# A float32-split encoder trunk on one core: branch B in another order, wider spacing of attention heads, the softmax scaling on another engine, two output blocks interleaved, and tiles written in the order in which the transposes read them

## The chip, the cores and the metric

The kernel runs on one core of one Trainium2 chip. The metric is the device time of one execution in microseconds (us), lower is better.

## The reference, cut to what matters

Two layers (DEPTH = 2), 256 tokens, 2048 channels, float32:

```python
h = rmsnorm(x, pre_norm_g[l])
proj = einsum('bsd,dn->bsn', h, w_in[l])       # 35 blocks of 512 columns
qa,ka,va, qb,kb,vb, qc,kc,vc, za,zb,zc, gates = split(proj)
ya = neighbourhood_attention(qa, ka, va, rpb[l])   # branch A: 8 heads
yb = gqa_attention(rope(rmsnorm(qb)), rope(rmsnorm(kb)), vb)  # branch B: 8 heads, 2 for k and v
yc = dilated_mixture(qc, kc, vc)                   # branch C: 12 heads, 4 sums
merged = ga*((ya*silu(za)) @ w_branch_a) + gb*((yb*silu(zb)) @ w_branch_b) \
       + gc*((yc*silu(zc)) @ w_branch_c)           # ga, gb, gc = sigmoid(gates + b_gate)
x = x + rmsnorm(merged @ w_out[l], post_norm_g[l])
```

## The kernel before, in words

**The stream of products.** All large products run as one list, `stream`, of steps (block, kc). A block (`Blk`) is one product with 512 output columns, and a step takes 256 of its input channels for all 256 tokens. For each step SP loads 512 KB of weights (`emit_raw`, L189), ScalarE rounds them to the fast float32 format (`emit_hi`, tile wh, L195), VectorE forms the remainder (`emit_lo`, tile wl, L200), and TensorE runs 12 matmuls of 128x512 (`run_half` and `mm3`, L170 to L172): two halves of the tokens (T = 0, 1), two groups of 128 channels, and three products each, wh by the high part, wl by the high part, wh by the low part. `ahead` issues the loads some six steps ahead, wh three and wl two steps ahead.

**The order of blocks of a layer.** z, q, k, v of branch C; z, q, k, v of branch A, twice; z of B (blocks 20, 21), k and v of B (8), q of B (6, 7); then four times `merge`: three gate blocks and the products by w_branch_a, w_branch_c and w_branch_b; then four output blocks (`out_block`) by w_out. An output block's steps kc = 0 to 7 read the merged tiles mT 0 to 3, two steps each.

**Everything else rides in slots.** After each step `slot()` is called once: it evacuates up to one finished accumulator, moves every active job (a Python generator) to its next `yield`, and may start one new job. Light jobs (`later`) go first; a heavy job, one attention head, starts only when no light job waits and the count `cool` that the head before has set is down to zero. Engines take their instructions in program order, so the slot in which a piece is issued sets what stands before and behind it on its engine.

**Turns.** Results come token-major (tokens on the partitions) and are needed channel-major. `turn` transposes 32x32 blocks on VectorE (L148, into tile tt), writes tt to DRAM and reads it back as tx (L153, L157 on SP, two slots apart each). The program has 168 such transposes: 88 of 128x512 that read q, k, z (tile tok) or the merged tile (g), less four of half the width, and 80 that read softmax results (tile sp). Each reads its source with a stride of four elements (`p (h b j) -> p h j b`). `tr_job` is a turn and the split of the result into a high and a low part. Of a turn's tiles the writers are: `evac_qk` (L326, ScalarE), `evac_z` (L353 ScalarE, L354 VectorE), `evac_p` (L605, L607 VectorE) for the merged tile, `softmax` (L369, exp on ScalarE) for p, and `rope` (L513, L521, L523) for q and k of branch B.

**A head** (`head_job`): six 128x256 matmuls into sc; `softmax`: maximum (L364), for B times a factor (L366), exp; one slot later `norm`: 1/sum (L377, L378) and p times it (L380, VectorE); two slots later the turn of p; after it the split into pp (L130, L132), two slots, six matmuls into o, and `gate` (L384). The last head of a group of four splits the result into yT. In branch B the heads are queued by the `then` of the `tr_job` of q, in the slot in which that job issues its last pieces. `evac_qb` evacuates q of B: squares of four heads (L531), a factor (L533), `rope`, L546.

## Time and profile before

| | |
|---|---|
| median of 3 runs | 2043.8 us (2043.03 to 2046.01) |
| the profiled execution | 2045.3 us; from its first to its last instruction 2043.2 us |
| mean granted TensorE clock | 0.994 of full speed |
| TensorE matmuls | 9098, busy 2014.1 us |
| VectorE busy | 1294.6 us (63%) |
| ScalarE busy | 959.0 us (47%) |
| mean HBM rate | 228 GB/s |

In the rows below, PE is TensorE, DVE is VectorE, ACT is ScalarE, SP issues the transfers. A group's row reads: line, engine, operation, out<-in, shapes, count | busy us, mean ns of one | idle time of the engine just before them and what ended it. A matmul's end is modelled: it is shown as 0.39 us long while the next one starts 0.23 us after it, so pace is read from starts and counts, and a gap shown is some 0.16 us shorter than what was lost.

### The profile page before, as it was taken

The page shows a single profiled execution, that of the slowest core. Times are in us where ns is not written, and L with a number is a line of the kernel's source. Part 1 is how long each engine was busy: PE and PEld are TensorE (multiplying, and loading weights), DVE is VectorE, ACT ScalarE, POOL GpSimd, SP SyncE. Part 2 cuts the span into 40 slices and gives each one's busy share as a digit, 9 for nine tenths or more (in the row PEclk, how much of TensorE's full clock was granted, in tenths as well). Part 3 has the DMA queues.
Part 4 walks back from the last instruction along what each step waited for, and adds up shares of the span by engine and source line. Part 5 has one row for each costly group of instructions (what it writes and reads, how often), then busy time and mean ns, then how long its engine had stood idle before and what let it go on. Part 6 is the DMA issues. An engine that isn't in the chain of part 4 may idle for free.

```text
span 2043.2 us, 24560 instructions
## 1 busy us (share of the span) xinstructions
PE 2014.1 (99%) x9098; PEld 1666.8 (82%) x9098; DVE 1294.6 (63%) x1645; ACT 959.0 (47%) x1402; POOL 24.0 (1%) x31
## 2 busy tenths in 40 slices
PE   9999999999999999999999999999999999999998
PEld 7888888888778888887888888888887788888876
DVE  6654587776786564645565555786767865646554
ACT  7544445445453444342564453555454544443422
POOL 0000000000000000000000000000000000000000
PEclk9999999999999999999999999999999999999999
DMA  8776375866666756667557664768665666656572
GB/s 326 258 263 258 137 287 203 290 215 257 217 215 225 263 199 218 226 212 272 185 167 275 240 249 144 277 226 303 211 259 191 240 217 245 217 195 225 201 283 72
DMA packets 171719, 468.05 MB, mean 229 GB/s; under 512 B 15440, under 2 KB 58576, under 8 KB 171600
## 3 DMA queue, kind: packets, MB, share of 16 engines
q1 hardware_dynamic: 171600, 466.50, 63.4%
q8 instruction: 71, 1.16, 0.2%
q14 instruction: 48, 0.39, 0.1%
HBM read 427.11 MB, written 39.32 MB: 228 GB/s over the span
## 4 chain that ended last, share of the span: by engine, by line
PE 89%; DVE 5%; ACT 2%; DMA 2%; issue 1%; SPq 0%; DVEq 0%; ACTq 0%; POOLq 0%
PE acc L171 29%; PE acc L172 29%; PE acc L170 29%; DMA tx<-turn 2%; DVE wl L200 1%; DVE tt L148 1%; ACT wh L195 1%; DVE nm L364 0%; ACT sp L369 0%; DVE pp L132 0%; PE sc L172 0%; PE sc L446 0%; DVE sp L380 0%; PE o L172 0%; PE o L171 0%
## 5 line engine op out<-in xcount | busy, mean ns | idle before, releaser
L200 DVE TENSOR_TENSOR wl<-raw,wh 128x1024 fp32r<-128x1024 f32 (+1 forms) x706 | 830.7, 1213 | 145.4 <-ACT wh L195 144.9
L171 PE MATMUL acc<-wl,hTh 128*128 128x512 f32 x2240 | 876.3, 391 | 7.4 <-DVE wl L200 7.4
L170 PE MATMUL acc<-wh,hTh 128*128 128x512 f32 x2240 | 877.4, 392 | 0.4 <-ACT wh L195 0.4
L172 PE MATMUL acc<-wh,hTl 128*128 128x512 f32 x2240 | 874.2, 390 | 0.0
L195 ACT CAST wh<-raw 128x1024 fp32r<-128x1024 f32 (+1 forms) x706 | 703.4, 1043 | 346.9 <-DMA raw<-in_wpack_dram 217.8
L171 PEld LDWEIGHTS acc<-wl,hTh 128*128 128x128 f32 x2240 | 422.2, 188 | 97.9 <-DVE wl L200 12.7
L172 PEld LDWEIGHTS acc<-wh,hTl 128*128 128x128 f32 x2240 | 422.1, 188 | 88.1
L170 PEld LDWEIGHTS acc<-wh,hTh 128*128 128x128 f32 x2240 | 422.3, 189 | 86.1 <-ACT wh L195 0.9
L170 PE MATMUL acc<-wh,yTh 128*128 128x512 f32 x320 | 124.5, 389 | 0.0
L171 PE MATMUL acc<-wl,yTh 128*128 128x512 f32 x320 | 124.5, 389 | 0.0
L172 PE MATMUL acc<-wh,yTl 128*128 128x512 f32 x320 | 124.5, 389 | 0.0
L594 ACT ACTIVATE g<-g 128x512 f32<-128x512 f32 x48 | 30.4, 634 | 192.8 <-DVE g L593 192.8
L593 DVE SCALAR_TENSOR_TENSOR g<-acc,rsx,bg 128x512 f32<-128x512 f32 x48 | 35.9, 747 | 128.7 <-PE acc L172 128.5
L170 PE MATMUL acc<-wh,mTh 128*128 128x512 f32 x256 | 101.6, 397 | 3.8 <-ACT mTh L130 3.8
L172 PE MATMUL acc<-wh,mTl 128*128 128x512 f32 x256 | 101.0, 395 | 0.0
L171 PE MATMUL acc<-wl,mTh 128*128 128x512 f32 x256 | 101.0, 394 | 0.0
L369 ACT ACTIVATE sp<-sp,nm 128x256 f32<-128x256 f32 (+1 forms) x48 | 27.6, 576 | 116.4 <-DVE nm L364 116.4
L605 DVE SCALAR_TENSOR_TENSOR g<-g,acc 128x512 f32<-128x512 f32 x48 | 32.8, 684 | 68.1 <-PE acc L172 68.1
L148 DVE STREAM_TRANSPOSE tt<-tok 128x512 f32<-128x512 f32 (+1 forms) x72 | 73.5, 1060 | 0.0
L171 PEld LDWEIGHTS acc<-wl,yTh 128*128 128x128 f32 x320 | 60.1, 188 | 12.4
L172 PEld LDWEIGHTS acc<-wh,yTl 128*128 128x128 f32 x320 | 60.1, 188 | 12.4
L170 PEld LDWEIGHTS acc<-wh,yTh 128*128 128x128 f32 x320 | 60.1, 188 | 12.3
(111 smaller groups left out, 1078.0 us busy)
## 6 DMA issues: line engine op xcount, KB each, us to landing
raw<-in_wpack_dram SPq DMA_DIRECT2D x558, 512.0 KB, 6.5
raw<-in_wo_dram SPq DMA_DIRECT2D x64, 512.0 KB, 9.2
turn<-tt SPq DMA_DIRECT2D x50, 512.0 KB, 3.0
tx<-turn SPq DMA_DIRECT2D x50, 512.0 KB, 5.5
raw<-in_wa_dram SPq DMA_DIRECT2D x32, 512.0 KB, 3.4
raw<-in_wb_dram SPq DMA_DIRECT2D x32, 512.0 KB, 4.6
turn<-tt SPq DMA_DIRECT2D x34, 256.0 KB, 2.2
tx<-turn SPq DMA_DIRECT2D x34, 256.0 KB, 4.3
```

The costliest lines, as they stand in the source:

```text
L148: nc.vector.transpose(out=tt[:, :, T].rearrange("p j (h a) -> p h j a", h=n), in_=srcs[T].rearrange("p (h b j) -> p h j b", h=n, j=4))
L170: nc.tensor.matmul(out_, lhsT=lh, rhs=rh, start=first, stop=False)
L171: nc.tensor.matmul(out_, lhsT=lh, rhs=rl, start=False, stop=False)
L172: nc.tensor.matmul(out_, lhsT=ll, rhs=rh, start=False, stop=last)
L195: nc.scalar.copy(HI[i][:, k], RAW[i][:, k])
L200: nc.vector.tensor_tensor(out=LO[i][:, k], in0=RAW[i][:, k], in1=f32(HI[i][:, k]), op=ALU.subtract)
L369: nc.scalar.activation(p[:, i], sc[:, i], AF.Exp, bias=nm[:, i:i + 1], scale=1.0 if f is None else f[:, i:i + 1], accum_out=sm[:, i:i + 1])
L593: nc.vector.scalar_tensor_tensor(g, ps, S["rs"][T], BG[i], op0=ALU.mult, op1=ALU.add)
L594: nc.scalar.activation(g, g, AF.Tanh, scale=0.5)
L605: nc.vector.scalar_tensor_tensor(G[i][:, T], G[i][:, T], 1.0, ps, op0=ALU.add, op1=ALU.mult)
```

## The change

1. Tiles that will be turned are written so that the transposes read them without a stride: `evac_qk`, `evac_z` and the exp of `softmax` write element 4q+j of a row to place j, q (`fourths` of the out, `plain` of the in), so consecutive elements land 128 elements (64 for a row of 256) apart. `turn` then reads `p (j q) -> p j q`. Of the merged tile the last sum writes in this order, into G[2] in place of G[0]. q and k of branch B are still written plainly and turned with the stride (`kept=False`).
2. p is multiplied by 1/sum on ScalarE (an activation Copy with a column as scale) instead of VectorE.
3. Heads of A and B set `cool` 3 instead of 2, heads of C 5 instead of 4. After the `tr_job` of q of B two more slots pass before its heads are queued.
4. Block 21 (z of the second half of B) moves from its place before k and v of B to the place between q blocks 6 and 7.
5. The first two output blocks run as: steps 0 to 5 of the first, steps 0 to 5 of the second, then steps 6, 7 of each. Accumulators are kept by block and half.

```diff
@@ -37,6 +37,8 @@
         self.far = False
+        self.mate = None
+        self.mated = False
         self.before = {}
@@ -140,13 +142,23 @@
-    def turn(srcs, n, tx):
+    def fourths(t):
+        return t.rearrange("p (j q) -> p q j", j=4)
+    def plain(t):
+        return t.rearrange("p (q j) -> p q j", j=4)
+    def turn(srcs, n, tx, kept=True):
         for T in range(2):
-            nc.vector.transpose(out=tt[:, :, T].rearrange("p j (h a) -> p h j a", h=n),
-                                in_=srcs[T].rearrange("p (h b j) -> p h j b", h=n, j=4))
+            if kept:
+                nc.vector.transpose(out=tt[:, :, T], in_=srcs[T].rearrange("p (j q) -> p j q", j=4))
+            else:
+                nc.vector.transpose(out=tt[:, :, T].rearrange("p j (h a) -> p h j a", h=n),
+                                    in_=srcs[T].rearrange("p (h b j) -> p h j b", h=n, j=4))
         run = 2 * n * 32
@@ -301,11 +313,11 @@
-        def tr_job(dst, tok, n=4, then=None):
+        def tr_job(dst, tok, n=4, then=None, kept=True):
             tx = []
-            yield from turn([tok[:, T] for T in range(2)], n, tx)
+            yield from turn([tok[:, T] for T in range(2)], n, tx, kept)
             for T in range(2):
@@ -314,6 +326,8 @@
             if then:
+                yield
+                yield
                 then()
@@ -323,7 +337,7 @@
                     store[key] = pair("qk", [4, 256]) if two else U("qkT", [4, 256])
-                nc.scalar.activation(tok[0][:, T], ps, AF.Copy, scale=S[which][T])
+                nc.scalar.activation(fourths(tok[0][:, T]), plain(ps), AF.Copy, scale=S[which][T])
                 if T == 1:
@@ -349,9 +363,9 @@
                     SZ[key] = U("z", [4, 256])
-                z = tok[0][:, T]
-                nc.scalar.activation(z, ps, AF.Tanh, scale=S["rsh"][T])
-                nc.vector.scalar_tensor_tensor(z, z, 1.0, ps, op0=ALU.add, op1=ALU.mult)
+                z = fourths(tok[0][:, T])
+                nc.scalar.activation(z, plain(ps), AF.Tanh, scale=S["rsh"][T])
+                nc.vector.scalar_tensor_tensor(z, z, 1.0, plain(ps), op0=ALU.add, op1=ALU.mult)
                 if T == 1:
@@ -366,7 +380,7 @@
             for i in range(n):
-                nc.scalar.activation(p[:, i], sc[:, i], AF.Exp, bias=nm[:, i:i + 1],
+                nc.scalar.activation(fourths(p[:, i]), plain(sc[:, i]), AF.Exp, bias=nm[:, i:i + 1],
                                      scale=1.0 if f is None else f[:, i:i + 1],
@@ -377,7 +391,7 @@
             for i in range(n):
-                nc.vector.tensor_scalar(p[:, i], p[:, i], r[:, i:i + 1], None, op0=ALU.mult)
+                nc.scalar.activation(p[:, i], p[:, i], AF.Copy, scale=r[:, i:i + 1])
@@ -489,7 +503,7 @@
                 for hh in range(4):
-                    heavy.append((2, job_a(u, hh, bias[hh // 2][:, hh % 2])))
+                    heavy.append((3, job_a(u, hh, bias[hh // 2][:, hh % 2])))
             proj(18 + u, evac_z(("a", u)))
@@ -545,8 +559,8 @@
                 if T == 1:
-                    later(tr_job(QT["b", u], tok[0],
-                                 then=lambda: heavy.extend((2, job_b(u, hh)) for hh in range(4))), 1)
+                    later(tr_job(QT["b", u], tok[0], kept=False,
+                                 then=lambda: heavy.extend((3, job_b(u, hh)) for hh in range(4))), 1)
             return f
@@ -565,13 +579,13 @@
             if T == 1:
-                later(tr_job(KT["b"], tok, n=2), 1)
+                later(tr_job(KT["b"], tok, n=2, kept=False), 1)
             for hh in range(4):
-                heavy.append((4, job_c(hh, dist)))
+                heavy.append((5, job_c(hh, dist)))
@@ -598,13 +612,16 @@
                 MT[nb] = pair("mT", [4, 256])
-                return tr_job(MT[nb], G[0])
+                return tr_job(MT[nb], G[2])
                     nc.vector.scalar_tensor_tensor(G[i][:, T], G[i][:, T], 1.0, ps, op0=ALU.add, op1=ALU.mult)
-                    if i:
-                        nc.vector.tensor_tensor(out=G[0][:, T], in0=G[0][:, T], in1=G[i][:, T], op=ALU.add)
+                    if i == 2:
+                        nc.vector.tensor_tensor(out=G[0][:, T], in0=G[0][:, T], in1=G[2][:, T], op=ALU.add)
+                    if i == 1:
+                        nc.vector.tensor_tensor(out=fourths(G[2][:, T]), in0=plain(G[0][:, T]), in1=plain(G[1][:, T]),
+                                                op=ALU.add)
                     if i == 1 and T == 1:
@@ -671,16 +688,18 @@
         a_unit(1)
-        proj(20, evac_z(("b", 0)))
-        b0 = proj(21, evac_z(("b", 1)))
+        b0 = proj(20, evac_z(("b", 0)))
         b0.at("after", (0, 1), b_tables)
         proj(6, evac_qb(0))
+        proj(21, evac_z(("b", 1)))
         proj(7, evac_qb(1))
             merge(nb)
-        for nb in range(4):
-            lastb = out_block(nb)
+        outs = [out_block(nb) for nb in range(4)]
+        outs[0].mate, outs[1].mated = outs[1], True
+        lastb = outs[3]
         lastb.lag = True
@@ -715,8 +734,12 @@
         for b in bl:
-            for kc in range(b.nc):
-                stream.append((b, kc))
+            if b.mate:
+                m = b.mate
+                stream += [(b, kc) for kc in range(6)] + [(m, kc) for kc in range(6)]
+                stream += [(c, kc) for c in (b, m) for kc in range(6, 8)]
+            elif not b.mated:
+                stream += [(b, kc) for kc in range(b.nc)]
@@ -756,7 +779,8 @@
         else:
-            order += [(i + k, T) for k in range(n) for T in range(2)]
+            n = 1
+            order += [(i, T) for T in range(2)]
         i += n
@@ -767,12 +791,12 @@
         if kc == 0:
-            ps[T] = mm.tile([P, 512], F32, name="acc")
-        run_half(i, T, ps[T])
+            ps[b, T] = mm.tile([P, 512], F32, name="acc")
+        run_half(i, T, ps[b, T])
         for f in b.after.get((kc, T), ()):
         if kc == b.nc - 1:
-            evq.append(b.evac(T, ps[T]))
+            evq.append(b.evac(T, ps.pop((b, T))))
         if T == 1 or b.lag:
```

What this moves is shown at three places, in the program's order of each engine; wl is the remainder of a step's weights, sc and o are a head's two products, nm its maximum.

VectorE in branch B of the first layer, around the split of the first q (`qkl`). Before (the rows ahead of qkl are the rope of the second q, tile tok with s):

```order
L521 TENSOR_TENSOR s<-acc,ropeg 128x8x32 x2
L523 TENSOR_TENSOR tok<-tok,s 128x512
L132 TENSOR_TENSOR qkl<-tx,qkh 128x4x128 x2
L364 TENSOR_REDUCE nm<-sc 128x2
L366 TENSOR_TENSOR nm<-nm,bf 128x2
L200 TENSOR_TENSOR wl<-raw,wh 128x1024
L546 TENSOR_SCALAR bf<-rs_y,rsx 128x4
L533 TENSOR_SCALAR hss<-hss,rsx 128x4
L513 TENSOR_TENSOR tok<-acc,ropeg 128x512
L377 RECIPROCAL rsum<-sm 128x2
L378 TENSOR_TENSOR rsum<-rsum,rsx 128x2
L380 TENSOR_SCALAR sp<-sp,rsum 128x256 x2
```

After, the same place:

```order
L134 TENSOR_TENSOR qkl<-tx,qkh 128x4x128 x2
L212 TENSOR_TENSOR wl<-raw,wh 128x1024
L368 SCALAR_TENSOR_TENSOR tok<-tok,acc 128x128x4
L212 TENSOR_TENSOR wl<-raw,wh 128x1024 x2
L158 STREAM_TRANSPOSE tt<-tok 128x4x128 x2
L212 TENSOR_TENSOR wl<-raw,wh 128x1024
L378 TENSOR_REDUCE nm<-sc 128x2
L380 TENSOR_TENSOR nm<-nm,bf 128x2
L212 TENSOR_TENSOR wl<-raw,wh 128x1024
L391 RECIPROCAL rsum<-sm 128x2
L392 TENSOR_TENSOR rsum<-rsum,rsx 128x2
L212 TENSOR_TENSOR wl<-raw,wh 128x1024 x2
```

Before, the maximum `nm` of the first head follows the split at once, and the rope of the second q lies on both sides of it. Now wl of four steps, the z of block 21 (tok<-tok,acc) and its transposes stand between the split and the first nm, and 1/sum is no longer followed by p's scaling on this engine. The rope of the second q now comes behind the second head's start, where VectorE has:

```order
L158 STREAM_TRANSPOSE tt<-sp 128x4x64 x2
L378 TENSOR_REDUCE nm<-sc 128x2
L380 TENSOR_TENSOR nm<-nm,bf 128x2
L212 TENSOR_TENSOR wl<-raw,wh 128x1024
L547 TENSOR_SCALAR hss<-hss,rsx 128x4
L527 TENSOR_TENSOR tok<-acc,ropeg 128x512
L535 TENSOR_TENSOR s<-acc,ropeg 128x8x32 x2
L537 TENSOR_TENSOR tok<-tok,s 128x512
L391 RECIPROCAL rsum<-sm 128x2
L392 TENSOR_TENSOR rsum<-rsum,rsx 128x2
L212 TENSOR_TENSOR wl<-raw,wh 128x1024
L560 TENSOR_SCALAR bf<-rs_y,rsx 128x4
```

ScalarE in the same branch, from one head's exp (`sp,sm<-sc,nm,bf`) to the next. Before:

```order
L369 ACTIVATE sp,sm<-sc,nm,bf 128x256 x2
L195 CAST wh<-raw 128x1024
L130 ACTIVATE pp<-tx 128x2x128 x2
L195 CAST wh<-raw 128x1024
L369 ACTIVATE sp,sm<-sc,nm,bf 128x256 x2
```

After:

```order
L383 ACTIVATE sp,sm<-sc,nm,bf 128x64x4 x2
L207 CAST wh<-raw 128x1024
L132 ACTIVATE pp<-tx 128x2x128 x2
L394 ACTIVATE sp<-sp,rsum 128x256 x2
L207 CAST wh<-raw 128x1024 x2
L383 ACTIVATE sp,sm<-sc,nm,bf 128x64x4 x2
```

p's scaling (`sp<-sp,rsum`) now stands on ScalarE, between the split of an earlier head (pp) and the next two casts wh; three casts of a step lie between two exps where there were two.

TensorE in the first layer's output blocks, where step 5 of the first block ends (numbers tell tiles apart: mTh_5507 is the merged tile 0, mTh_6841 tile 2, mTh_7510 tile 3). Before:

```order
L170 MATMUL acc_7501<-wh_7540,mTh_6841 128x512
L171 MATMUL acc_7501<-wl_7560,mTh_6841 128x512
L172 MATMUL acc_7501<-wh_7540,mTl_6842 128x512
L170 MATMUL acc_7494<-wh_7558,mTh_7510 128x512
L171 MATMUL acc_7494<-wl_7580,mTh_7510 128x512
L172 MATMUL acc_7494<-wh_7558,mTl_7511 128x512
```

After:

```order
L182 MATMUL acc_7505<-wh_7540,mTh_6841 128x512
L183 MATMUL acc_7505<-wl_7560,mTh_6841 128x512
L184 MATMUL acc_7505<-wh_7540,mTl_6842 128x512
L182 MATMUL acc_7622<-wh_7558,mTh_5507 128x512
L183 MATMUL acc_7622<-wl_7580,mTh_5507 128x512
L184 MATMUL acc_7622<-wh_7558,mTl_5508 128x512
```

Before, the next matmul reads tile 3, which the four merge blocks finish last. Now a second pair of accumulators takes tiles 0 to 2 first, 72 matmuls, before any matmul reads tile 3.

## Rows read from the trace of the kernel before

**Rows 1.** The page, part 1: busy us (share of the span) and instructions by engine.

```profile
PE 2014.1 (99%) x9098; PEld 1666.8 (82%) x9098; DVE 1294.6 (63%) x1645; ACT 959.0 (47%) x1402; POOL 24.0 (1%) x31
```

**Rows 2.** Windows of TensorE: stretch and its us, busy us (count), granted clock, DMA share, GB/s.

```profile
530.00:630.00 100.00, 93.54 (x443) 0.98 0.69 243
640.00:920.00 280.00, 280.00 (x1237) 1.00 0.61 215
930.00:955.00 25.00, 23.04 (x93) 0.93 0.87 319
...
1535.00:1635.00 100.00, 94.24 (x428) 0.95 0.61 217
1945.00:1970.00 25.00, 23.18 (x94) 0.93 0.77 281
```

**Rows 3.** The same, of the products by weights (tile acc) alone.

```profile
530.00:630.00 100.00, 83.24 (x347) 0.98 0.69 243
1535.00:1635.00 100.00, 85.30 (x344) 0.95 0.61 217
```

**Rows 4.** Timeline of TensorE, two matmuls of a head: start us, us, instruction.

```profile
538.33 0.28 PE L170 MATMUL sc<-kb,qkh 128*128 128x256 f32 x1
538.45 0.27 PE L171 MATMUL sc<-kb,qkh 128*128 128x256 f32 x1
```

**Rows 5.** Waits of TensorE, whole span: us in total, times, longest us.

```profile
PE acc L171 <- DVE wl L200: 7.4, 11, 2.0
PE acc L170 <- ACT mTh L130: 3.8, 2, 2.0
```

**Rows 6.** Chain of waits, 930 to 947 us: start us, us, what.

```profile
935.54 8.55 DMA tx<-turn
...
946.90 0.43 PE acc L170
```

**Rows 7.** Windows of all engines in branch B, first layer.

```profile
560.00:600.00 40.00, 39.22 (x197) 32.92 (x196) 34.34 (x71) 21.73 (x47) 0.00 (x0) 1.00 0.70 238
```

**Rows 8.** Groups of VectorE by shape.

```profile
L200 DVE TENSOR_TENSOR wl<-raw,wh 128x1024 fp32r<-128x1024 f32 x702 | 827.9, 1216 | 145.2 <-ACT wh L195 144.7 <-issue 0.3
L148 DVE STREAM_TRANSPOSE tt<-tok 128x512 f32<-128x512 f32 x68 | 71.2, 1086 | 0.0
L148 DVE STREAM_TRANSPOSE tt<-sp 128x256 f32<-128x256 f32 x64 | 37.2, 620 | 0.0
...
L132 DVE TENSOR_TENSOR pp<-tx,pp 128x256 fp32r<-128x256 f32 x80 | 31.0, 425 | 16.7 <-ACT pp L130 14.4 <-DMA raw<-in_wpack_dram 2.2
L607 DVE TENSOR_TENSOR g<-g 128x512 f32<-128x512 f32 x32 | 22.1, 692 | 1.1
...
L380 DVE TENSOR_SCALAR sp<-sp,rsum 128x256 f32<-128x256 f32 x64 | 19.7, 351 | 1.1
L384 DVE TENSOR_TENSOR z<-o,z 128x256 f32<-128x256 f32 x40 | 16.8, 421 | 32.2 <-PE o L172 22.0 <-PE o L476 10.2
...
L364 DVE TENSOR_REDUCE nm<-sc 128x2 f32<-128x512 f32 x16 | 11.0, 687 | 2.5 <-PE sc L172 2.5
...
L513 DVE TENSOR_TENSOR tok<-acc,ropeg 128x512 f32<-128x512 f32 x8 | 5.5, 685 | 0.0
```

**Rows 9.** Groups of ScalarE by shape.

```profile
L195 ACT CAST wh<-raw 128x1024 fp32r<-128x1024 f32 x702 | 700.9, 1045 | 346.7 <-DMA raw<-in_wpack_dram 217.8 <-DMA raw<-in_wo_dram 41.7 <-PE acc L171 30.1
...
L130 ACT ACTIVATE pp<-tx 128x256 fp32r<-128x256 f32 x80 | 29.7, 411 | 32.0 <-DMA tx<-turn 19.8 <-DVE z L384 4.3 <-DMA raw<-in_wpack_dram 3.7
L326 ACT ACTIVATE tok<-acc,rsx 128x512 f32<-128x512 f32 x40 | 27.4, 685 | 67.6 <-PE acc L172 67.6
...
L369 ACT ACTIVATE sp<-sc,nm,bf 128x256 f32<-128x256 f32 x32 | 17.8, 560 | 47.8 <-DVE nm L366 47.8
...
L566 ACT ACTIVATE tok<-tok,kf 128x128 f32<-128x128 f32 x8 | 2.8, 395 | 7.3 <-DVE kf L563 7.3
```

**Rows 10.** Timeline of VectorE: the wait behind the squares of q.

```profile
543.76 0.23 DVE L533 TENSOR_SCALAR hss<-hss,rsx 128x4 f32<-128x4 f32 x1 [2.46 <-ACT junk L531]
```

## The prediction, made before the change was run

> **What bounds the kernel now.** I read the engines' totals first: TensorE is busy 99% of the span [rows 1], no other engine over 63%, so only time in which TensorE does not run at its pace can be won. Its pace is in the long undisturbed stretch from 640 to 920 us: 1237 matmuls of 128x512 in 280 us, 0.2264 us each [rows 2]. A matmul of half that width starts 0.12 us before the next one [rows 4]. Laid over the disturbed stretches, this gives what is lost in them. Neither that pace nor the number of matmuls is touched by the change.
>
> *Branch B.* The stretch 530 to 630 us holds 443 matmuls, 347 of them products by weights [rows 2, 3]; the other 96 are those of heads. 347 x 0.2264 + 96 x 0.12 = 90.1, so 9.9 of 100 us are lost. In the second layer (1535 to 1635 us): 344 x 0.2264 + 84 x 0.12 = 88.0, 12.0 lost. Together 21.9 us.
>
> *The first output block.* 930 to 955 us holds 93 matmuls, 21.1 us of work: 3.9 lost. 1945 to 1970 holds 94, 21.3: 3.7 lost [rows 2]. Together 7.6 us.
>
> What ended the waits: TensorE waits most for wl, VectorE's remainder of the weights, and next for mTh, the merged tile (2.0 us at most) [rows 5]. Idle time is only about half of such a loss: the granted clock over these 25 us is 0.93 [rows 2], and in the chain of waits a matmul behind the wait takes 0.43 us [rows 6], nearly twice the pace. A wait of 2 us is followed by a spell at the lower level (1.2 instead of 2.4 GHz) that costs about as much again; it goes when the wait goes.
>
> In branch B VectorE is the bound: from 560 to 600 us it is busy 34.3 of 40 us [rows 7], and wl is late because it stands in program order behind the work of heads. The work of a head on VectorE, from [rows 8], small [128x2] pieces left out: maximum 0.69, p's scaling 2 x 0.35, transposes 2 x 0.62, split 2 x 0.425, gate 0.42, sum 3.90 us. Heads start two slots apart: two steps take 24 x 0.2264 + 12 x 0.12 = 6.87 us on TensorE, and VectorE needs 3.90 + 2 x 1.216 = 6.33, 92%, before the rope and the gates' evacuation. So it falls behind.
>
> **The change, part by part.**
>
> *Output blocks interleaved.* The matmuls that need tile 3 come 72 matmuls later, 72 x 0.2264 = 16.3 us. What is waited for is the read-back of the turn, 8.55 us in flight [rows 6], and TensorE waited 2.0 us for it [rows 5]; 16 us cover it eight times over. I take all 7.6 us. Moved with it: the second block's bias and x loads are issued two steps earlier, ahead of that turn on SP instead of behind it, which shortens the burst behind the turn. Late next would be the second block's weights (a rival below).
>
> *Order and spacing in branch B.* Three steps per head take 36 x 0.2264 + 1.44 = 9.59 us; at the old prices VectorE would need 3.90 + 3.65 = 7.55, 79%. Two slots more ahead of the first head put four wl between the split of q and the first maximum, where there was none, so the first sc no longer stands right behind the split. Block 21 now stands between the two q blocks, so the second rope comes a block later, after the first two heads have started and not on top of the first. The price: eight heads end later. The last gate is issued three steps before the first matmul that reads its yT, 8.2 us against gate 0.42, ScalarE's and VectorE's split of 128x1024 (about 1.0 and 1.2, as wh and wl [rows 8, 9]): covered.
>
> *p's scaling on ScalarE.* Off VectorE: 0.70 us a head. ScalarE has no row of a scaled copy of 256 elements; one of 128 takes 0.395, one of 512 from an accumulator 0.685 [rows 9], so 0.49 by the line between. It is 0.1 to 0.2 dearer there, on an engine with room: per head three wh 3.14, exp 1.12, split 0.82, scaling 0.98, 6.1 of 9.59 us. The Trainium skill (ScalarE: Activation LUTs, section "Rules for kernel authors") wants multiplications on VectorE; by it the scaling stays there and a head costs VectorE 0.70 more, 7% of the pace, which the sum would hardly show.
>
> *Reads without stride.* A transpose of 128x512 takes 1.086 us, an ordinary pass over as many elements 0.692; for 256, 0.620 against 0.425 [rows 8]. Bounds for a stride-free one: 1.086 (nothing won) and 0.692. I take 0.692, since 0.77 ns an element is what the plain passes lack. 92 of 512 and 64 of 256 gain 36 + 12 = 48 us of VectorE, of which only those in branch B count: 0.39 a head. Then a head needs 3.90 - 0.70 - 0.39 = 2.81, with three wl 6.46 of 9.59 us, 67%.
>
> In return ScalarE (q, k, z, exp) and VectorE (z, the merged sum) write with gaps of 512 or 256 bytes. No row shows such a write. Bounds: nothing, or as four instructions of a quarter each, 4 x 0.395 - 0.685 = 0.9 us per 512 elements [rows 9]; nearest is the strided read, 0.39, which I take. On ScalarE in B that makes 6.5 (at the upper bound 7.0) of 9.59: covered, and evacuations have a whole block of 22 us. If that cover failed, wh would be late, then wl. The Trainium skill (SBUF — State Buffer, section "Door 1: The DMA port swizzle") says that consecutive accesses to one 16-byte line run at full rate and each move to another line pays. By this the transposes gain, which fits their rows, and the new writers pay as well; it gives no amount, and the sum stays as it is while ScalarE has room.
>
> *What is left in B.* The densest piece is the second rope with two heads: six steps, 6 x 2.72 + 1.4 = 17.7 us on TensorE, while VectorE has six wl 7.3, the rope's six passes at 0.69 4.1 and some 1.2 of small pieces, one maximum 0.69, one turn 0.85, one split 0.85, and q's two transposes, still strided, 2.2: 17.2, 97%. Ahead of the rope it also waits for ScalarE's squares, 2.46 us before [rows 10]. Against this stands the lead of wl, two steps or 5.4 us. So between nothing and 3 us a layer may stay; I leave 1.5 each.
>
> **Sum.** 7.6 + 21.9 - 3.0 = 26.5 us off the profiled execution's 2045.3 (span 2043.2) makes 2018.8. That execution is 1.5 above the median of 2043.8, so **2017.3** against the median. Start, tail and the step between layers are not touched.
>
> **The rivals.**
>
> 1. *All of it goes*, and smaller waits near branch A as well, since every stretch has less VectorE work: 29.5 and one or two more, 2013. For it: 67% instead of 92%. Against: the 97% piece.
> 2. *Half of B stays*, because the piece at 97% outruns the 5.4 us lead, or the scaling, now behind wh and the squares on ScalarE, makes p late: 2043.8 - 7.6 - 11 = 2025. For it: in-order engines with longer chains across two of them; against: 8 us of lead of wh.
> 3. *The turns get no cheaper* (the change does not do what it says), 1.086 staying: VectorE 71% in B instead of 67%, perhaps 1 us a layer more: 2019.
> 4. *A transfer takes the place of mTh*: in 930 to 955 us transfers run at 319 GB/s, 0.87 busy [rows 2], and without the wait the weights of the next steps are due 4 us earlier. If they are late by that, the 7.6 are given back: 2025. Against: the burst is shorter now.
> 5. *Slower: gapped writes make ScalarE the bound.* Place: exp in branches A and B, 512 elements a head, 16 heads a layer. ScalarE has 9.59 - 6.1 = 3.5 us to spare per head; beyond 6.8 ns an element each head is held up, and from 8.6 ns (4.4 us, 0.92 over, times 32 heads = 29.5) all gain is gone. At 10 ns: 1.6 x 32 = 51, 2043.8 - 29.5 + 51 = 2065. Against it: the strided read costs 0.77 ns, the upper bound 1.8. The line rule of the Trainium skill named above (SBUF — State Buffer) is what would make it so.
>
> **How the numbers follow.** Forecast 0.45, rival 1 0.17, 2 0.17, 3 0.12, 4 0.06, 5 0.03. The range runs from rival 1 with a margin, 2011.5, past rivals 2 and 4 to 2027; left out are rival 5 and the far ends of 2 and 4. A measurement of this kernel tells 0.2%, 4.1 us, from no change; all cases but rival 5 and a mixture of 2 and 4 lie far below that: faster 0.95, within 0.02, slower 0.03.
>
> **What would show it.** The windows of the output blocks at 0.2264 us a matmul and a granted clock of 1.00, with no wait for mTh; VectorE's transposes of tok, g and sp near 0.69 and 0.43 while those of B's q and k stay at 1.09 and 0.62; ScalarE's rows of q, z and exp longer by 0.2 to 0.4; a row of some 0.5 for the scaling; VectorE's busy share in B down to about 0.7, and TensorE's losses there at most 3 us a layer. Wrong I would be if TensorE waits for wh in B (ScalarE the bound), for weights in the output blocks, or if B still loses 5 us or more a layer.

## The result, and the profile after

The changed kernel takes 2022.4 us in the median of 5 runs (2020.91 to 2022.95); the kernel before, on the same chip, 2043.0 us (2040.70 to 2046.01; five runs, of which three gave the 2043.8 above). The ratio is 0.9896, 95% interval 0.9882 to 0.9911: 20.7 us faster. The forecast was 2017.3, range 2011.5 to 2027. The profiled execution took 2021.6 us, its span is 2019.5 where it was 2043.2: 23.7 us less, of the 26.5 that the prediction's sum takes off that execution.

The page of the changed kernel, part 1, which answers to [rows 1]:

```profile
PE 2002.7 (99%) x9098; PEld 1660.2 (82%) x9098; DVE 1237.2 (61%) x1565; ACT 1035.0 (51%) x1482; POOL 20.4 (1%) x31
```

VectorE lost 57 us of work, ScalarE took on 76, TensorE has as many matmuls as before. Next its windows of TensorE, columns as in [rows 2]:

```profile
530.00:630.00 100.00, 98.27 (x471) 1.00 0.68 239
640.00:920.00 280.00, 280.00 (x1237) 1.00 0.62 216
930.00:955.00 25.00, 25.00 (x112) 1.00 0.93 359
1535.00:1635.00 100.00, 98.38 (x473) 1.00 0.68 236
1945.00:1970.00 25.00, 25.00 (x112) 1.00 0.67 232
```

In the undisturbed stretch the pace is the same, 1237 matmuls in 280 us. In the output blocks 112 matmuls start in 25 us where there were 93 and 94: nothing is lost in these windows (the program is some microseconds further on in them than before; the table below has the blocks whole). In branch B of the two layers 471 and 473 start in 100 us where there were 443 and 428. The granted clock is 1.00 everywhere. Of these matmuls the products by weights are 381 and 383:

```profile
530.00:630.00 100.00, 89.16 (x381) 1.00 0.68 239
1535.00:1635.00 100.00, 89.27 (x383) 1.00 0.68 236
```

By the prediction's own working 381 x 0.2264 + 90 x 0.12 = 97.1, so 2.9 us of the first stretch are lost, and 2.5 of the second. VectorE's share in B, columns as in [rows 7], fell to 0.73 (0.86 before), near the 0.7 that the prediction named as a sign:

```profile
560.00:600.00 40.00, 39.89 (x195) 33.30 (x194) 29.18 (x54) 26.72 (x49) 0.00 (x0) 1.00 0.68 236
```

What TensorE still waits for, whole span, columns as in [rows 5]:

```profile
PE acc L183 <- DVE wl L212: 5.6, 12, 1.2
PE acc L89 <- DVE warm L86: 1.5, 1, 1.5
PE acc L182 <- ACT wh L207: 0.5, 1, 0.5
```

The wait for mTh is gone; that for wl fell only from 7.4 to 5.6 us. Three more waits are gone that the kernel before had and that neither [rows 5] nor the prediction lists:

```profile
PE sc L172 <- DVE qkl L132: 3.7, 2, 1.8
PE sc L170 <- ACT qkh L130: 1.8, 2, 0.9
PE o L171 <- DVE pp L132: 1.7, 2, 0.9
```

All three lie in branch B and are waits for a head's own inputs, 7.2 us together. The waits for wl in B were 4.9 us before and are 3.0 now. So most of the waiting that B lost was not for wl.

Groups by shape that answer to [rows 8, 9]:

```profile
L340 ACT ACTIVATE tok<-acc,rsx 128x512 f32<-128x512 f32 x40 | 48.2, 1204 | 70.5 <-PE acc L184 70.5
...
L158 DVE STREAM_TRANSPOSE tt<-tok 128x512 f32<-128x512 f32 x60 | 39.0, 690 | 0.0
...
L394 ACT ACTIVATE sp<-sp,rsum 128x256 f32<-128x256 f32 x64 | 29.1, 501 | 20.2 <-DVE rsum L392 20.2
L158 DVE STREAM_TRANSPOSE tt<-sp 128x256 f32<-128x256 f32 x64 | 24.4, 420 | 0.0
L383 ACT ACTIVATE sp<-sc,nm,bf 128x256 f32<-128x256 f32 x32 | 23.7, 818 | 56.7 <-DVE nm L380 56.7
```

Transposes fell from 1086 to 690 ns and from 620 to 420. Writers with gaps rose: `evac_qk` from 685 to 1204, exp from 560 to 818. The row of p's scaling (L394) is the important one. Its own 29 us are harmless; the 20.2 us in which ScalarE stands still ahead of it, because VectorE has not yet computed 1/sum (rsum), are new.

**Where the loss is.** The starts of all matmuls, measured against the pace (0.2264 and 0.12 us) and added up by stretch, give what TensorE loses between its first and its last matmul. Us, layer 1 / layer 2; "rest" is the start, branch C and the step between the layers:

| kernel | A | B | output blocks | rest | all |
|---|---|---|---|---|---|
| before | 1.6 / 1.4 | 9.9 / 11.9 | 4.1 / 3.9 | 7.6 | 40.5 |
| changed | 1.8 / 2.0 | 2.9 / 2.4 | 0 / 0 | 7.7 | 16.8 |

40.5 - 16.8 = 23.7, the whole difference of the spans. 8.0 us came from the output blocks, 16.5 from B. A lost 0.8 more, although VectorE has less work there.

**The mechanism, read from the changed kernel's timelines.** ScalarE in branch A (start us, us, instruction, in brackets idle time and what ended it):

```profile
350.63 1.17 ACT L367 ACTIVATE tok<-acc,rsx 128x512 f32<-128x512 f32 x1
351.59 0.72 ACT L132 ACTIVATE pp<-tx 128x256 fp32r<-128x256 f32 x2
353.95 0.91 ACT L394 ACTIVATE sp<-sp,rsum 128x256 f32<-128x256 f32 x2 [1.64 <-DVE rsum L392]
354.77 1.04 ACT L207 CAST wh<-raw 128x1024 fp32r<-128x1024 f32 x1
355.71 1.16 ACT L367 ACTIVATE tok<-acc,rsx 128x512 f32<-128x512 f32 x1
```

VectorE in the same microseconds:

```profile
351.83 1.10 DVE L368 SCALAR_TENSOR_TENSOR tok<-tok,acc 128x512 f32<-128x512 f32 x1 [2.33 <-ACT tok L367]
352.83 0.75 DVE L134 TENSOR_TENSOR pp<-tx,pp 128x256 fp32r<-128x256 f32 x2
353.50 0.16 DVE L391 RECIPROCAL rsum<-sm 128x2 f32<-128x2 f32 x1
353.69 0.16 DVE L392 TENSOR_TENSOR rsum<-rsum,rsx 128x2 f32<-128x2 f32 x1
353.77 1.22 DVE L212 TENSOR_TENSOR wl<-raw,wh 128x1024 fp32r<-128x1024 f32 x1
356.90 1.10 DVE L368 SCALAR_TENSOR_TENSOR tok<-tok,acc 128x512 f32<-128x512 f32 x1 [1.91 <-ACT tok L367]
357.91 1.20 DVE L212 TENSOR_TENSOR wl<-raw,wh 128x1024 fp32r<-128x1024 f32 x1
```

The engines wait for each other in turn. VectorE stands 2.33 us for tok (ScalarE's tanh of z); only then can it compute rsum; ScalarE stands 1.64 us for rsum; its next tok is late by that, and VectorE stands 1.91 us again. Neither is short of time. The last wl of this chain, ready at 359.1, makes a matmul 0.39 us late. In B it is the same with the squares of q (junk) in place of tok, and rsum there stands behind the rope. ScalarE:

```profile
538.58 0.20 ACT L545 ACTIVATION_READ_ACCUMULATOR junk<-acc 128x1 f32 x1
541.33 0.91 ACT L394 ACTIVATE sp<-sp,rsum 128x256 f32<-128x256 f32 x2 [2.55 <-DVE rsum L392]
542.14 1.03 ACT L207 CAST wh<-raw 128x1024 fp32r<-128x1024 f32 x1
543.08 0.27 ACT L545 ACTIVATE junk<-acc 128x128 f32<-128x128 f32 x1
```

Behind the wait stand a cast and the squares of the other half. VectorE stands 2.10 us for those, its wl comes after, and TensorE has its longest wait after the start:

```profile
544.67 0.23 DVE L547 TENSOR_SCALAR hss<-hss,rsx 128x4 f32<-128x4 f32 x1 [2.10 <-ACT junk L545]
...
545.40 1.22 DVE L212 TENSOR_TENSOR wl<-raw,wh 128x1024 fp32r<-128x1024 f32 x1
...
546.67 0.50 PE L183 MATMUL acc<-wl,hTh 128*128 128x512 f32 x1 [1.18 <-DVE wl L212]
```

### The profile page after: what moved, and what is told of

Same layout as the page of the kernel before. It is cut to its first block, busy times and chain, and to the rows that moved or that the text cites. A ratio compares the mean times of both kernels' runs of the same rounds, so it can differ in the third digit from the quotient of the medians.

```text
span 2019.5 us, 24536 instructions
## 1 busy us (share of the span) xinstructions
PE 2002.7 (99%) x9098; PEld 1660.2 (82%) x9098; DVE 1237.2 (61%) x1565; ACT 1035.0 (51%) x1482; POOL 20.4 (1%) x31
## 4 chain that ended last, share of the span: by engine, by line
PE 92%; DVE 3%; ACT 3%; DMA 1%; issue 1%; SPq 0%; DVEq 0%; POOLq 0%; ACTq 0%
PE acc L183 30%; PE acc L184 30%; PE acc L182 29%; DVE wl L212 1%; ACT wh L207 1%; DMA tx<-turn 1%; DMA raw<-in_wpack_dram 1%; PE sc L184 0%; PE sc L183 0%; PE sc L182 0%; ACT tok L367 0%; ACT junk L545 0%; PE o L184 0%; PE o L183 0%; PE o L182 0%
## 5 line engine op out<-in xcount | busy, mean ns | idle before, releaser
L383 ACT ACTIVATE sp<-sp,nm 128x256 f32<-128x256 f32 (+1 forms) x48 | 42.0, 926 | 116.8 <-DVE nm L378 116.8
L340 ACT ACTIVATE tok<-acc,rsx 128x512 f32<-128x512 f32 x40 | 48.2, 1204 | 70.5 <-PE acc L184 70.5
```

What stands on the lines that cost most here:

```text
L340: nc.scalar.activation(fourths(tok[0][:, T]), plain(ps), AF.Copy, scale=S[which][T])
L383: nc.scalar.activation(fourths(p[:, i]), plain(sc[:, i]), AF.Exp, bias=nm[:, i:i + 1], scale=1.0 if f is None else f[:, i:i + 1], accum_ou ...
```

## The experiments

The theory after this reading: p's scaling on ScalarE makes two engines that work in program order wait for each other; that costs what is left in A and B. Rivals: the gapped writes, as ScalarE's longer work, cost it; or the cheaper turns or the wider spacing are what holds the gain together. The kernels ran in three groups, each beside the kernel before on a chip of its own: 1 to 4 (before: 2045.75 us), 5 to 8 (2046.97), 9 to 11 (2046.23). A ratio is to the kernel before of the same group. One and the same kernel, the changed one, has 0.9896 above and 0.9883 in experiment 9, so a difference under some 3 us between groups tells nothing by itself. Losses by branch, from the same sum of starts, stand in one table behind the experiments.

**1. The scaling back on VectorE.**

```diff
-                nc.scalar.activation(p[:, i], p[:, i], AF.Copy, scale=r[:, i:i + 1])
+                nc.vector.tensor_scalar(p[:, i], p[:, i], r[:, i:i + 1], None, op0=ALU.mult)
```

> The changed kernel with p's scaling back on VectorE, everything else kept. Theory (the new waits for wl near branch A come from two in-order engines waiting for each other: ScalarE's scaling waits for 1/sum, the casts wh stand behind it): in the two stretches of branch A where the changed kernel loses 0.4 to 0.7 us at a time (350 to 490 and 1360 to 1490 us, some 3.6 us together) the loss falls under 1 us; branch B, where VectorE gets 0.7 us a head back, loses 0 to 2 us a layer more than its 2.9 and 2.4. Time 2020 to 2024 us against 2022.4. Rival (the gapped writes alone make the evacuations late): the waits of branch A stay at 3 us or more and branch B grows, 2024 to 2027.

Measured: 2015.9 us, ratio 0.9854 (0.9839 to 0.9869), better than either expected. A loses 0.1 a layer, B 1.2 and 1.4: not more, though VectorE has 0.70 us a head more to do. By the medians the scaling's move costs 6.5 us, by the spans 5.9 (2019.5 and 2013.6); the gapped writes, still in, do not by themselves make A lose.

**2. Turns with the stride, writers without gaps; the scaling stays on ScalarE.**

```diff
     def fourths(t):
-        return t.rearrange("p (j q) -> p q j", j=4)
+        return t
     def plain(t):
-        return t.rearrange("p (q j) -> p q j", j=4)
+        return t
...
-            if kept:
+            if False:
```

> The changed kernel with plain writes and strided transposes everywhere, as before the change; order, spacing, scaling on ScalarE and interleaving kept. Theory (the saving on the transposes is given back by the gapped writes, of which those on ScalarE stand in front of wh): ScalarE's evacuations fall back to 0.69 us, the waits of branch A fall to 1 us or less, branch B loses 1 to 2 us a layer more; 2020 to 2025 us, so within 3 us of the changed kernel. Rival (VectorE bounds branch B and needs the cheaper turns): branch B loses 5 us or more a layer, 2027 us or more.

Measured: 2019.8 us, ratio 0.9875 (0.9862 to 0.9889), a little better than the theory's range. A falls to 0.8 and 0.3, B rises to 3.3 and 3.8, in the first layer by less than expected. ScalarE's wait for 1/sum is nearly as long as in the changed kernel:

```profile
L394 ACT ACTIVATE sp<-sp,rsum 128x256 f32<-128x256 f32 x64 | 29.0, 501 | 18.2 <-DVE rsum L392 18.2
```

So in A it takes both, the wait and the long gapped writes in the chain behind it: without either of them A loses little. While the scaling stands on ScalarE in that slot the layout gains nothing: the kernel is 2.6 us faster without it by the medians, 4.3 or 1.6 by the ratios, and the same by the profiled spans (2019.7 and 2019.5; the profiled execution is the slowest of this kernel's four).

**3. Output blocks one after the other.**

```diff
-        outs[0].mate, outs[1].mated = outs[1], True
```

> The changed kernel with the output blocks one after the other again. Theory (the wait for the last merged tile and the low clock behind it are 3.9 and 3.7 us and nothing takes their place): both waits come back in full, 93 or 94 matmuls in 25 us around the first output block, granted clock 0.93 there, 2029 to 2031 us. Rival (a transfer has taken part of the gain in the changed kernel): less than 5 us come back, under 2027.5.

Measured: 2028.8 us, ratio 0.9918 (0.9904 to 0.9932): 6.4 us slower than the changed kernel by the medians, 4.5 by the ratios, 7.2 by the spans. The wait is back in this kernel's trace:

```profile
PE acc L182 <- ACT mTh L132: 4.5, 2, 2.3
```

and the first layer's window shows both parts of the loss, idle time and clock (two windows of 20 us):

```profile
920.00:940.00 20.00, 17.80 (x78) 0.98 0.67 220
940.00:960.00 20.00, 20.00 (x84) 0.93 1.03 403
```

The output blocks lose 4.1 and 2.9 us. The interleaving is worth about what was forecast.

**4. Heads at the old spacing, scaling on ScalarE.**

```diff
-                    heavy.append((3, job_a(u, hh, bias[hh // 2][:, hh % 2])))
+                    heavy.append((2, job_a(u, hh, bias[hh // 2][:, hh % 2])))
```

(in the same way 3 to 2 for B and 5 to 4 for C)

> The changed kernel with heads two steps apart again (four for branch C). Theory (VectorE's work per head has fallen from 3.90 to 2.81 us, with two wl 5.2 of 6.9 us, 76%, so the wider spacing is no longer needed once turns and scaling are off VectorE): branch B loses at most 2 us a layer more, 2022 to 2026 us. Rival (the spacing is what removed the waits): branch B loses 4 us or more a layer above the changed kernel, 2030 us or more.

Measured: 2033.5 us, ratio 0.9943 (0.9931 to 0.9956). The spacing is worth 11 us here by the medians, but less than half of it in B: A, for which nothing had been expected, loses 5.3 and 5.4. B loses 1.9 and 2.4 more, the theory's size and not the rival's, but the time is the rival's, and "76% busy leaves room" fell.

**5. 1/sum in one slot, the scaling on ScalarE one slot later.** `norm` is split in two, and the second half takes the place of the first of the two empty slots, so p's turn is issued in the slot in which it was:

```diff
-            norm(p, sm, 2, S["rsh2"])
+            r = inverse(sm, 2, S["rsh2"])
             yield
+            scale(p, r, 2)
             yield
```

> The changed kernel with p's scaling still on ScalarE but issued one slot after 1/sum on VectorE (heads of A and B; the turn stays in its slot). Theory A (the scaling costs because ScalarE stands still for 1/sum, which VectorE reaches late, and the casts wh queue behind it): with a slot between them the wait is gone, the losses fall from 1.8 and 2.0 us in branch A to under 0.6 and in B from 2.9 and 2.4 to under 1.8; 2016 to 2018.5 us. Rival (ScalarE's added work and the longer way from p to the turn cost, whenever it is issued): A stays at 1.5 us or more and B at 2.3 or more a layer, 2021 to 2024 us.

Measured: 2014.0 us, ratio 0.9839 (0.9826 to 0.9853), the lowest of all and below the range of either theory. Work, engine and layout are those of the changed kernel; only the place in ScalarE's order differs. A loses 0.1 a layer, B 0.4. Its row of the scaling:

```profile
L400 ACT ACTIVATE sp<-sp,rsum 128x256 f32<-128x256 f32 x64 | 28.8, 498 | 0.3 <-DVE rsum L395 0.2
```

As many instructions as long as before, with 0.3 us of waiting ahead of them in place of 20.2. Its ScalarE at the place in branch A that was shown above (all is 1.52 us later here):

```profile
353.11 0.72 ACT L132 ACTIVATE pp<-tx 128x256 fp32r<-128x256 f32 x2
353.73 1.04 ACT L207 CAST wh<-raw 128x1024 fp32r<-128x1024 f32 x1
354.67 1.19 ACT L367 ACTIVATE tok<-acc,rsx 128x512 f32<-128x512 f32 x1
355.65 0.87 ACT L400 ACTIVATE sp<-sp,rsum 128x256 f32<-128x256 f32 x2
```

Cast and tok go ahead while 1/sum is on its way. What TensorE waits for in this kernel:

```profile
PE acc L182 <- ACT wh L207: 1.1, 1, 1.1
PE acc L183 <- DVE wl L212: 1.0, 4, 0.4
```

All but 0.3 us of these lies in the start of the program, which loses 1.5 us more in this execution than in the changed kernel's.

**6. Scaling on VectorE and heads at the old spacing** (1 and 4 together).

> Scaling on VectorE and heads two steps apart (four in C), the rest as changed. Theory (the 11 us that the narrow spacing cost with the scaling on ScalarE are the two engines' mutual waits at a higher rate): with the scaling on VectorE most of them are gone, 2017 to 2021 us against 2015.9 with wide spacing. Rival (the spacing itself is needed: VectorE has 3.90 - 0.39 + 2.43 = 5.9 us of work in 6.9 with two steps a head, 86%, before rope and gates): 4 us or more a layer come back, 2024 us or more.

Measured: 2028.8 us, ratio 0.9916 (0.9902 to 0.9929): 12.7 us above experiment 1 by the ratios. The rival was right: the spacing is needed wherever the scaling stands; A and B lose 6.7 and 9.0 us a layer.

**7. Scaling on VectorE, branch B in the old order.** Block 21 goes back ahead of block 8, and the two slots ahead of the heads of B go:

```diff
-        b0 = proj(20, evac_z(("b", 0)))
+        proj(20, evac_z(("b", 0)))
+        b0 = proj(21, evac_z(("b", 1)))
...
-        proj(21, evac_z(("b", 1)))
...
             if then:
-                yield
-                yield
                 then()
```

> Scaling on VectorE, and block 21 back before k and v of B and the two extra slots before B's heads taken out. Theory (the first head's products stand right behind the split of q again and the second rope falls on the first heads): branch B loses 3 us or more a layer above its 1.2 and 1.4, 2021 to 2025 us. Rival (with wide spacing and cheaper turns VectorE has enough room, the order no longer matters): 2016 to 2018.5 us.

Measured: 2032.7 us, ratio 0.9928 (0.9916 to 0.9941): 15 us above experiment 1 by the ratios, twice what was expected. Its waits of TensorE:

```profile
PE sc L184 <- DVE qkl L134: 3.5, 2, 1.8
PE acc L182 <- ACT yTh L132: 3.3, 2, 1.7
PE acc L183 <- DVE wl L212: 3.3, 5, 1.5
PE sc L182 <- ACT qkh L132: 1.9, 2, 1.0
```

Without the two slots the first sc stands right behind the split of q, and the waits for qkl and qkh are back at what they were in the kernel before (3.7 and 1.8). And the spacing of three slots, in the old order, pushes the last gate of B against the first product that reads its yT, a wait that the kernel before did not have. A and B of both layers lose 24.8 us in the kernel before, 17.0 here with the new spacing alone, 15.7 in experiment 6 with the new order alone and 2.8 in experiment 1 with both. Each alone gains 8 or 9 us, the two together 22: they help each other. (The kernel before also has the strided turns, which the next experiment finds worth nothing.)

**8. Scaling on VectorE, turns with the stride** (1 and 2 together).

> Scaling on VectorE, plain writes and strided transposes, so only order, spacing and interleaving of the change remain. Theory (the turns' saving counts in branch B, where VectorE is short, and the gapped writes lie beside other work): B loses 1 to 2 us a layer more than 1.2 and 1.4, branch A stays under 0.5; 2017 to 2020 us against 2015.9. Rival (the saving is worth nothing once the heads are spaced, and the gapped writes cost a little): 2013 to 2016 us.

Measured: 2016.3 us, ratio 0.9849 (0.9836 to 0.9863), the same as experiment 1: the rival's range, just missed, and not the theory's.

**9. The changed kernel once more**, beside the next two.

> The changed kernel once more, beside the runs below and on the same chip, so that they compare without a change of chip. Expected: the same losses as in its first run within 0.6 us a branch (A 1.8 and 2.0, B 2.9 and 2.4), and a time 5 to 9 us above the version whose scaling comes a slot later.

Measured: 2022.2 us, ratio 0.9883 (0.9867 to 0.9900). Its losses are 2.2 / 1.6 in A and 2.5 / 3.2 in B. The second layer's B is 0.8 us off, more than the 0.6 expected: between executions a branch's loss wanders by that much, while the sum of the four stays (9.5 against 9.1).

**10. The scaling one slot later, heads at the old spacing** (5 and 4 together).

> Scaling on ScalarE one slot after 1/sum, and heads two steps apart (four in C). Theory (the narrow spacing costs because VectorE and ScalarE each meet two heads' pieces per two steps and fall behind in order, whichever has the scaling): A and B together lose 5 us or more a layer, 2023 us or more. Rival (the narrow spacing cost so much only through waits for 1/sum, and VectorE's 5.2 of 6.9 us per head leave room): at most 2 us a layer, 2014 to 2018 us.

Measured: 2024.8 us, ratio 0.9897 (0.9880 to 0.9913). With the old spacing, too, the later slot is worth 9 us (2033.5 in experiment 4), and the spacing is still worth 12 us by the ratios of 5 and 10. The theory holds in the main (A and B lose 4.3 and 6.2 us a layer). The longest wait of the first layer, on TensorE (PE), and what VectorE (DVE) did ahead of it:

```profile
545.80 0.23 DVE L554 TENSOR_SCALAR hss<-hss,rsx 128x4 f32<-128x4 f32 x1 [2.69 <-ACT junk L552]
...
547.46 1.22 DVE L212 TENSOR_TENSOR wl<-raw,wh 128x1024 fp32r<-128x1024 f32 x1
...
548.74 0.50 PE L183 MATMUL acc<-wl,hTh 128*128 128x512 f32 x1 [2.19 <-DVE wl L212]
```

Here VectorE stood idle for 2.69 us, waiting for ScalarE's squares of q, until 1.7 us before it began the wl that came late. It was not short of time; that wl stood behind other pieces in its order.

**11. The scaling one slot later, turns with the stride** (5 and 2 together).

> Scaling on ScalarE one slot after 1/sum, plain writes and strided transposes. Theory (the transposes' 48 us of VectorE lie beside other work once heads are spaced, and so do the gapped writes): within 1.5 us of the version with gapped writes, 2012.5 to 2015.5 us, branch B at most 1 us a layer. Rival (the cheaper turns are worth something in branch B): B loses 1.5 us or more a layer above 0.4, 2017 us or more.

Measured: 2014.2 us, ratio 0.9843 (0.9825 to 0.9862), the same as experiment 5. So the layout for the turns is worth nothing that these runs could tell. It takes 48 us off the transposes; VectorE's own gapped writes give some back, and its busy time differs by 36 us (1271.1 here, 1234.9 in experiment 5).

Losses of TensorE in us, layer 1 / layer 2, and the medians:

| kernel | A | B | output blocks | all | median, us |
|---|---|---|---|---|---|
| 1 scaling on VectorE | 0.1 / 0.1 | 1.2 / 1.4 | 0 / 0 | 11.2 | 2015.9 |
| 2 strided turns | 0.8 / 0.3 | 3.3 / 3.8 | 0 / 0 | 17.1 | 2019.8 |
| 3 no interleaving | 1.8 / 1.6 | 2.5 / 2.5 | 4.1 / 2.9 | 23.9 | 2028.8 |
| 4 old spacing | 5.3 / 5.4 | 4.8 / 4.8 | 0 / 0 | 29.3 | 2033.5 |
| 5 scaling a slot later | 0.1 / 0.1 | 0.4 / 0.4 | 0 / 0 | 10.1 | 2014.0 |
| 6 = 1 + 4 | 3.5 / 3.0 | 3.2 / 6.0 | 0 / 0 | 24.1 | 2028.8 |
| 7 = 1, old order of B | 1.8 / 1.4 | 7.6 / 6.2 | 0 / 0 | 25.9 | 2032.7 |
| 8 = 1 + 2 | 0.1 / 0.1 | 1.7 / 1.4 | 0 / 0 | 11.7 | 2016.3 |
| 10 = 5 + 4 | 1.8 / 2.1 | 2.5 / 4.1 | 0 / 0 | 19.4 | 2024.8 |
| 11 = 5 + 2 | 0.1 / 0.1 | 1.2 / 0.5 | 0 / 0 | 9.8 | 2014.2 |

## Why the prediction was right, and which step failed

- **"Output blocks interleaved"**: right. 7.6 us were taken, 8.0 came by the sums of starts; undone alone (experiment 3) it costs 6.4 by the medians, 4.5 by the ratios, 7.2 by the spans. Rival 4 did not happen: the transfers moved 359 GB/s in 930 to 955 us and no weight was late.
- **"Order and spacing in branch B"**: right that it carries most, 16.5 us of B's 21.8. The reason was incomplete. I priced it as a share of VectorE that falls from 92% to 79%, with wl late. But experiments 4, 6 and 10, with VectorE's work cut, lose 4.3 to 10.2 us a layer in A and B at the old spacing: what is lost there is order, not the engine's sum, and in experiment 10 the late wl follows an idle stretch of VectorE. And 7.2 us of the waits that went were not for wl but for a head's own inputs (qkl, qkh, pp), the first two of which are back when the order is undone (experiment 7). I took the order for an extra; experiments 6 and 7 show that it and the spacing help each other.
- **"p's scaling on ScalarE"**: this step failed. I costed it at nothing, since ScalarE has 6.1 us of work in 9.59, and its duration was right (0.501 against 0.49). Not priced was the wait that the change adds: the scaling needs 1/sum from VectorE, and on ScalarE everything behind it waits along, casts wh first. It costs 7.0 us by the spans of the profiled executions (2019.5 and 2012.5 in experiment 5), 8.4 by the medians, and 8.1 of the 9.1 us that are left in A and B by the table; experiments 9 and 11, on one chip, differ by 8.1 too (11 has the strided turns as well, worth nothing there). Rival 2 had the mechanism by half ("the scaling, now behind wh and the squares on ScalarE, makes p late"): not p was late but what stands behind the scaling. The Trainium skill (ScalarE: Activation LUTs, section "Rules for kernel authors") puts multiplications on VectorE. As a choice between the two engines in that slot it agrees with experiment 1, which is faster, and VectorE's scaling is the shorter (351 ns there against 501). But the speed per element, which the rule gives as its reason, is not what decided, for in experiment 5 ScalarE multiplies and the kernel is as fast or faster.
- **"Reads without stride"**: the prices were right on VectorE (0.690 and 0.420) and short on ScalarE (0.52 us more per 512 elements, 0.39 taken, bound 0.9). The value was not: experiments 8 and 11 put the whole item at nothing with the new spacing (with the old one it was not tried). The 67% of the sum did not matter, since VectorE is not short of time once the heads are spaced. The writers with gaps pay, as the rule of the Trainium skill cited in the prediction (SBUF — State Buffer, section "Door 1: The DMA port swizzle") has it for consecutive accesses to other lines. Rival 5 is far: 1.0 ns an element against the 6.8 from which it would begin.
- **"What is left in B"**: 1.5 us a layer were left, 2.9 and 2.4 measured, 2.3 more; and A, which the sum left as it was, lost 0.8 more than before. Those two, less 0.4 that the output blocks gave beyond the forecast, make 2.7 of the 2.8 us by which the profiled execution missed. That it missed by no more is in part luck: the 3.0 us were kept for the 97% piece, the second rope with two heads, and in experiment 5 that piece is there and B loses 0.4 a layer. The allowance covered part of a cost of the scaling, for which it was not made. Without that cost the time is 2014.0, next to rival 1 (2013).
- **The sum.** 26.5 us were taken off the profiled execution, which would have been 2018.8; it was 2021.6, 2.8 more. The rest of the 5.1 us between 2017.3 and 2022.4 is reference: I set the median 1.5 below the profiled execution, as it was before, and it lies 0.8 above it.

What of this is argued, not shown: that the longer gapped writes lengthen the chain in A (experiment 2 fits it, yet its B moved as well); that order alone makes the late wl in A at the old spacing, where no timeline was read; and how much of experiment 7 belongs to block 21 and how much to the two slots, which were not tried apart.

**The best version** is experiment 5, 2014.0 us; with strided turns (experiment 11) it is as fast. Against the kernel before it gains 33 us, and of the 10.1 us that TensorE still loses, 9 are the start, branch C and the step between the layers. Experiment 1 (2015.9) lies within what two groups can differ by; its trace loses 1.1 us more.

## What to carry to other kernels

When an operation moves to an engine with room, ask not only what it takes there but what it waits for, and what stands behind it in that engine's order: two engines that are each half idle can still hold each other up by waiting in turn. The remedy cost nothing here: issue the dependent operation one slot later than its input, so that other ready work stands between. And before saving an engine's time, look whether that engine's sum or only its order makes the bound engine wait.

## What the runs showed of the hardware

- **Gaps cost the writer more than the reader.** An fp32 row of 512 written with gaps took ScalarE 1204 ns instead of 685 and exp 1254 instead of 724, 1.0 ns an element; VectorE's sum of the merged tile rose from 692 to 1096, 0.8 ns. The strided read by the transpose cost 0.77 ns an element.
- **Which waits brought the clock down.** Before, with waits of 2.0 us, five windows of 20 us have a granted clock of 0.83 to 0.91. In the changed kernel, whose longest wait between matmuls after the start is 1.2 us, no window from 100 to 2000 us is below 1.00. In experiment 4 (longest wait 2.7 us) two are, in experiment 7 one (0.92):

```profile
540.00:560.00 20.00, 17.31 (x71) 0.91 0.52 172
...
1560.00:1580.00 20.00, 17.32 (x78) 0.91 0.81 265
```

(these two are of experiment 4). Experiment 7 also has a wait of 1.8 us in the second layer behind which no window fell, and experiment 6 one of 2.9 us in the first layer, so the length of a single wait does not decide it alone.
